# Hybrid RG-LRU, attention and FFN layer: eighth gate pair in Strassen's form, first q and k ahead of the pairs, last gate product behind the second k

## The chip, the cores and the metric

The kernel runs on one core of one Trainium2 chip. The metric is device time in microseconds (us). Before the change three runs took 919.93, 920.62 and 920.92 us; the median is 920.62. The engines are TensorE (PE; PEld is its loading of weights), VectorE (DVE), ScalarE (ACT), GpSimd (POOL) and SyncE (SP). In this kernel SP issues most loads and stores, and POOL the transfers that accumulate.

## The reference

One layer, on x of 512 tokens by 1024 channels in float32. What matters here:

```
h  = RMSNorm_pre(x)
[xa, ga, q, k, v, f, gA, gB] = h @ W_in
A  = GeLU(ga) * RG-LRU(CausalDWConv4(xa))            (width 1280)
B  = ForgettingAttention(q, k, v, f)                 (16 heads of 64)
m  = sigmoid(gA) * (A @ P_A) + sigmoid(gB) * (B @ P_B)
x  = x + RMSNorm_post(m @ W_out)
h  = RMSNorm_pre(x)
u  = CausalDWConv3(h @ W_up); y = (GeLU(u_gate) * u_val) @ W_down
x  = x + RMSNorm_post(y)
```

The attention is causal; the score of token i against token j has the sum of log-sigmoids of f between them added.

## The kernel before

Values are kept transposed, with channels on the 128 partitions and the 512 tokens along the free dimension. Each matmul of float32 accuracy is made of three of the rounded type float32r: a value is split into a rounded part (`wh` of a weight, `hh` of h) and the rest (`wl`, `hl`), and wh by hh (line 218), wh by hl (line 219) and wl by hh (line 220) are accumulated. `project` computes an output tile of 128 channels by 512 tokens in 8 x 3 = 24 such matmuls of 128x512. A weight's path: SP loads it (`raw`, line 166), ACT rounds it (`wh`, line 172), DVE subtracts (`wl`, line 175). `fetch(i)` does this for all weights of a list, `order`, up to number i, `unit(name, ahead)` for the named one and `ahead` more. Four buffers each stand behind raw, wh and wl.

Each of the two gates has eight tiles, ma0 to ma7 for gA and mb0 to mb7 for gB. A gate tile ends with a tanh on ACT (line 865). That of ma is then multiplied into `pa`, the product A @ P_A, on DVE; that of mb is stored to DRAM by SP (`gmb`, line 873) and loaded again much later.

Fourteen of the sixteen tiles are computed in pairs, class `Pair`, with Strassen's seven products (Winograd's form) in place of eight: two tiles are a matrix of two by two blocks (two output tiles, two halves of the 1024 channels), against two halves of the tokens. A product has 12 matmuls of 128x256: 4 wh by rounded h (line 414), 4 wh by the rest of h (line 415) and 4 wl by rounded h (line 417). Products 1, 2 and 3 take plain weights, of which `plain_high` rounds the high part on ACT (`gmh`, line 369); the low part `gml` comes from `plain_low`, which writes the negative high part on ACT (line 360) and lets a transfer of POOL add the raw weight to it (line 361). Products 4 to 7 take sums of weights: `sums` on DVE (`gt`), `sums_hi` rounds them on ACT (`gth`, line 396), `sums_lo` subtracts on DVE (`gtl`). `keep` copies a product out of PSUM on ACT (`gx`, line 421), `add` adds it to another on DVE (line 433). On TensorE a period of one pair has its products 5 and 6, the product 4 of the pair before, its product 3, products 1 and 2 of the next pair, and its product 7. So the last pair leaves one product 4 behind.

Before the pairs, mb6 and mb7 are computed as plain tiles (`gate_tile`). Behind the pairs come q0, k0, the last pair's product 4, and the attention: eight steps p of two heads each. `scores(p)` is a set of matmuls of 64 partitions, two at a time (line 987), each in three rounds (high by high, low k, low q). Its six PSUM banks are read on DVE, which adds the bias B and takes the row maximum (line 996); ACT takes the exponential (line 1001), and `normalise` scales by the reciprocal sum on DVE (lines 1008, 1011). In the code of a step follow the projection of q(p+1), the transposes `pt` of step p-1, the projection of k(p+1), and the product with v, `av`, of step p-1. `halves` splits q and k: h_q and h_k on ACT (line 973), l_q and l_k on DVE (line 974). The bias B is broadcast from DRAM by POOL (line 893) and masked there (line 898).

PSUM has eight banks of 128x512, given out in turn. What sets the order: the code of the gate pairs stands in `manual_schedule`, so there each engine executes its instructions as they are written, up to the last product 4. Outside of it, the framework's scheduler puts each engine's instructions in an order. An engine goes through its own queue in order; `behind` ties the fetch of a weight to the last rounding of `halves`.

Of the kernel before, what the change touches and what calls it, by code (L numbers as in the profile page):

```python
# [19 lines left out]
KD = D // P  # L20
# [43 lines left out]
def kernel(  # L64
# [34 lines left out]
    def bank(name):  # L99
        return pspools[-1].tile([P, 512], F32, tag="ps", name=name)  # L100
# [79 lines left out]
    def cols(w, i):  # L180
        return w[i], (KD, P)
# [5 lines left out]
    order += [(f"v{c}_{u}", w_in[B_V + 4 * c + u], (2, 512)) for c in range(2) for u in range(4)]  # L187
    order += [(f"ga{t}", *cols(w_in, B_GA + t)) for t in range(TR)]
    order += [(f"pa{e}_{i}", w_pa[2 * e + i], (5, P)) for e, i in PA_ORDER]
    order += [(f"mb{e}", *cols(w_in, B_MB + e)) for e in (6, 7)]  # L190
    for p in range(KD):
        order.append((f"q{p}", *cols(w_in, B_Q + p)))
        order.append((f"k{p}", *cols(w_in, B_K + p)))
# [5 lines left out]
    where = {name: i for i, (name, _, _) in enumerate(order)}  # L199
    ready, emitted, special = {}, [0], {}  # L200

    def fetch(i):
        while emitted[0] <= min(i, len(order) - 1):
            n, src, shape = order[emitted[0]]
            w = Split(src, shape, n, special.get(n))
            w.hi()
            w.lo(dve)
            ready[n] = w.parts()
            emitted[0] += 1

    def unit(name, ahead=2):

        i = where[name]
        fetch(i + ahead)
        return ready.pop(name)
# [6 lines left out]
    def project(dst, unit, ah, al, lo=0, hi=S):  # L222
        wh, wl = unit
        for k in range(KD):
            mm3(dst[:, lo:hi], wh[:, k], wl[:, k], ah[:, k, lo:hi], al[:, k, lo:hi], k == 0, k == KD - 1)
# [256 lines left out]
    with ExitStack() as rg:  # L482
# [327 lines left out]
        gdram = ctx.enter_context(tc.tile_pool(name="gdram", bufs=1, space=bass.MemoryType.DRAM))  # L810
        gmb = [gdram.tile([P, S], F32, name=f"gmb{e}") for e in range(KD)]
        gates = Halved("g", lambda e: w_in[(B_MA if e[:2] == "ma" else B_MB) + int(e[2])], hh, hl)
        GP = [(f"{w}{e}", f"{w}{e + 1}") for w, n in (("ma", 8), ("mb", 6)) for e in range(0, n, 2)]
        gp = {}
        dstk = mstk.enter_context(ExitStack())
        sumstk, hfstk, splitstk, bstk = (ExitStack() for _ in range(4))
# [45 lines left out]
    def gate_tanh(name, ps):  # L862
        c = int(name[2]) + (0 if name[:2] == "ma" else KD)
        tg = tgpool.tile([P, S], F32, tag="tg", name=f"tg_{name}")
        act.activation(out=tg, in_=ps, func=AF.Tanh, scale=0.5, bias=hb[:, c : c + 1])
        return tg

    def gate_use(name, tg):
        e = int(name[2])
        if name[:2] == "ma":  # L870
            dve.scalar_tensor_tensor(out=pa[:, e], in0=tg, scalar=1.0, in1=pa[:, e], op0=ALU.add, op1=ALU.mult)
        else:
            nc.sync.dma_start(gmb[e], tg)

    def gate_tile(name, ahead):
        pg = bank(name)
        project(pg, unit(name, ahead), hh, hl)
        gate_use(name, gate_tanh(name, pg))

    def gate_epilogue(b, which, step):  # L880
        if b and step < 2:
            name = b.tiles[which == "c"]
            if step == 0:
                b.tg = getattr(b, "tg", {})
                b.tg[which] = gate_tanh(name, getattr(b, which))
            else:
                gate_use(name, b.tg[which])
# [11 lines left out]
                                   pattern=[[-1, P]], channel_multiplier=1)  # L899
        return bias  # L900

    gate_tile("mb6", 1)
    gate_tile("mb7", 0)
    with ExitStack() as g2:
        spool = g2.enter_context(tc.tile_pool(name="gsums", bufs=1, side="right", reuse_waits="tile"))
        gates.sh = [spool.tile([P, KH, SH], F32R, name=f"gsh{i}") for i in range(4)]
        gates.sl = [spool.tile([P, KH, SH], F32R, name=f"gsl{i}") for i in range(4)]
        gp[1] = Pair(gates, 1, GP[1])
        man = g2.enter_context(ExitStack())
        man.enter_context(tc.manual_schedule())  # L910
        for i, f in enumerate((fq[3], fq[0], fq[2], fq[1])):
            act.copy(gates.sh[i], f)
            sub(gates.sl[i], f, gates.sh[i].bitcast(F32))
        hfstk.close()
        st0pool = splitstk.enter_context(tc.tile_pool(name="gsplit0", bufs=2, side="right", reuse_waits="tile"))
        offset(splitstk, 448, "right")
        st1pool = splitstk.enter_context(tc.tile_pool(name="gsplit1", bufs=2, side="right", reuse_waits="tile"))
        gates.stpools = [st0pool, st1pool]
        none = Nothing()
        p, n = gp[0], gp[1]  # L920
        p.plain_high(0)
        p.plain_high(1)
        p.p12()
        p.p5()
        n.sums(0)
        n.sums(1)
        n.plain_low(0)
        p.keep(2, p.a[:, Y])
        p.add(p.a[:, X], p.a[:, X], 2)
        p.keep(1, p.c[:, X])  # L930
        n.sums_hi(0)
        n.sums_lo(0)
        n.sums_hi(1)
        n.sums_lo(1)
        n.plain_high(0)
        gp[2] = Pair(gates, 2, GP[2])

        def more(j):
            if j + 3 < len(GP):
                gp[j + 3] = Pair(gates, j + 3, GP[j + 3])  # L940
            elif j + 2 < len(GP):
                pass
            else:
                fetch(where[("q0", "k0")[j + 2 - len(GP)]])

        for j in range(len(GP)):
            period(gp[j], gp.get(j - 1), gp.get(j + 1, none), gp.get(j + 2, none), gate_epilogue, lambda: more(j))
            gp.pop(j - 1, None)
        splitstk.close()
        sumstk.close()  # L950
        bpool = bstk.enter_context(tc.tile_pool(name="bias", bufs=2, reuse_waits="tile"))
        bias = prep_alloc(0)
        b = gp.pop(len(GP) - 1)
        b.add(b.c[:, Y], b.a[:, Y], 1)
        b.add(b.c[:, X], b.c[:, X], 0)
        gate_epilogue(b, "c", 0)
        pq = bank("q0")
        project(pq, unit("q0", 0), hh, hl)
        gate_epilogue(b, "c", 1)
        pk = bank("k0")  # L960
        project(pk, unit("k0", 0), hh, hl)
        b.product(4, b.a[:, Y])
        gate_epilogue(b, "a", 0)
        gate_epilogue(b, "a", 1)

    with ExitStack() as at:
        at.enter_context(bstk)
# [98 lines left out]

        rounded = []

        def behind(name):
            with tc.issue_after(rounded[-1].ins):  # L1070
                return unit(name)

        q, k = halves(pq, "q0"), halves(pk, "k0")
        fetch(where["k1"])
        prev = None
        for p in range(KD):
            now = scores(p, q, k, bias)
            if p < KD - 1:
                bias = prep_alloc(p + 1)
                pq = bank(f"q{p + 1}")  # L1080
                project(pq, (unit if p else behind)(f"q{p + 1}"), hh, hl)
            else:
                pb_part(0, range(KD - 2))
            if prev is not None:
                pts = pt(p - 1, prev)
            if p < KD - 1:
                pk = bank(f"k{p + 1}")
                project(pk, behind(f"k{p + 1}"), hh, hl)
                q, k = halves(pq, f"q{p + 1}"), halves(pk, f"k{p + 1}")
            else:  # L1090
                pb_part(1, range(KD - 2))
            if prev is not None:
                av(p - 1, pts)
            normalise(now)
            prev = now
# [612 lines left out]
```

## Time and profile before

| | |
|---|---|
| median of three runs | 920.62 us (919.93 to 920.92) |
| profiled execution | 919.7 us |
| its span | 917.9 us |
| granted TensorE clock, mean | 0.998 |
| TensorE busy | 905.9 us |
| VectorE, ScalarE, GpSimd busy | 721.9, 597.7, 215.8 us |
| mb6 and mb7, plain | 248.27 to 259.15 us |
| first start of the pairs' products | 259.15 us |
| q0 begins, last product 4 begins, scores 0 begins | 327.21, 338.33, 339.86 us |

The profile is one profiled execution; its times count from the start of its span. A line of its timeline has the start, the duration, the engine, the source line, the operation with its output and inputs, and in brackets the idle time of the engine ahead of it with what ended it. TensorE's matmuls overlap, and their ends are modelled, so the time that one takes on the engine is read from the distance of two starts.

### The profile page before, as it was taken

The page shows a single profiled execution, that of the slowest core. Times are in us where ns is not written, and L with a number is a line of the kernel's source. Part 1 is how long each engine was busy: PE and PEld are TensorE (multiplying, and loading weights), DVE is VectorE, ACT ScalarE, POOL GpSimd, SP SyncE. Part 2 cuts the span into 40 slices and gives each one's busy share as a digit, 9 for nine tenths or more (in the row PEclk, how much of TensorE's full clock was granted, in tenths as well). Part 3 has the DMA queues.
Part 4 walks back from the last instruction along what each step waited for, and adds up shares of the span by engine and source line. Part 5 has one row for each costly group of instructions (what it writes and reads, how often), then busy time and mean ns, then how long its engine had stood idle before and what let it go on. Part 6 is the DMA issues. An engine that isn't in the chain of part 4 may idle for free.

```text
span 917.9 us, 15845 instructions
## 1 busy us (share of the span) xinstructions
PE 905.9 (99%) x5870; PEld 803.2 (88%) x5870; DVE 721.9 (79%) x1190; ACT 597.7 (65%) x1034; POOL 215.8 (24%) x279
## 2 busy tenths in 40 slices
PE   8999999999999999999999999999999999999997
PEld 7988888878899987888888889999999999978886
DVE  5966369638767647888868588899999999889897
ACT  7555495433467646677654477788888888677664
POOL 4134345444111112112104200132323223100000
PEclk9999999999999999999999999999999999999999
DMA  7767689989877776235424654378888888799764
GB/s 276 241 209 210 166 207 250 273 218 194 195 184 184 182 260 247 104 126 179 143 83 153 205 185 158 93 194 208 219 230 214 238 199 211 222 372 326 243 204 147
DMA packets 71760, 187.07 MB, mean 204 GB/s; under 512 B 7233, under 2 KB 27761, under 8 KB 71298
## 3 DMA queue, kind: packets, MB, share of 16 engines
q1 hardware_dynamic: 47648, 127.72, 41.9%
q0 software_dynamic: 23888, 58.20, 29.0%
q8 instruction: 46, 0.75, 0.3%
q14 instruction: 32, 0.26, 0.1%
q10 hardware_dynamic: 146, 0.14, 0.0%
HBM read 150.69 MB, written 35.73 MB: 203 GB/s over the span
## 4 chain that ended last, share of the span: by engine, by line
PE 89%; DMA 4%; DVE 4%; issue 1%; ACT 1%; POOL 0%; SPq 0%; DVEq 0%; ACTq 0%; POOLq 0%
PE up L417 7%; PE up L414 6%; PE up L415 6%; PE dn L1420 4%; PE dn L1418 4%; PE dn L1419 4%; DMA ml<-raw_up 2%; PE ga L218 2%; PE ga L219 2%; PE ga L220 2%; PE q L218 2%; PE k L218 2%; PE pb L218 2%; PE wo L1142 2%; PE k L220 2%; PE pb L219 2%
## 5 line engine op out<-in xcount | busy, mean ns | idle before, releaser
L1300 DVE SCALAR_TENSOR_TENSOR u<-up,cpt,u 128x511 f32<-128x511 f32 x96 | 71.2, 744 | 2.6 <-ACT u L1294 0.9
L361 POOL DMA_DIRECT2D ml<-raw_up x41 | 35.2, 858 | 154.2 <-ACT ml L360 91.1
L1418 PE MATMUL dn<-wh_dn,ah 128*128 128x512 f32 (+1 forms) x180 | 67.6, 376 | 0.2 <-ACT ah L1386 0.2
L1420 PE MATMUL dn<-wh_dn,al 128*128 128x512 f32 (+1 forms) x180 | 67.7, 376 | 0.0
L1419 PE MATMUL dn<-wl_dn,ah 128*128 128x512 f32 (+1 forms) x180 | 67.6, 375 | 0.0
L414 PE MATMUL up<-sh,th 128*128 128x256 f32 x252 | 60.2, 276 | 0.0
L415 PE MATMUL up<-sl,th 128*128 128x256 f32 x252 | 60.2, 276 | 0.0
L175 DVE TENSOR_TENSOR wl_dn<-raw_dn,wh_dn 128x1024 fp32r<-128x1024 f32 x42 | 51.5, 1226 | 9.2 <-ACT wh_dn L172 9.1
L172 ACT CAST wh_dn<-raw_dn 128x1024 fp32r<-128x1024 f32 x42 | 44.1, 1050 | 17.8 <-issue 8.0
L325 DVE TENSOR_TENSOR tl<-t,th 128x1024 fp32r<-128x1024 f32 x42 | 51.0, 1217 | 0.0
L1294 ACT ACTIVATE u<-up,cpt 128x512 f32<-128x512 f32 x48 | 37.0, 779 | 21.4 <-PE up L417 11.6
L415 PEld LDWEIGHTS up<-sl,th 128*128 128x128 f32 x252 | 47.3, 188 | 0.0
L414 PEld LDWEIGHTS up<-sh,th 128*128 128x128 f32 x252 | 47.3, 188 | 0.0
L396 ACT CAST th<-t 128x1024 fp32r<-128x1024 f32 x42 | 43.8, 1045 | 3.8 <-DVE t L325 0.8
L1308 POOL TENSOR_TENSOR yf<-u,u 128x512 f32<-128x512 f32 x23 | 29.9, 1298 | 63.6 <-issue 44.0
L414 PE MATMUL up<-h2h,mh 128*128 128x256 f32 x168 | 40.2, 276 | 0.0
L415 PE MATMUL up<-h2l,mh 128*128 128x256 f32 x168 | 40.2, 276 | 0.0
L1420 PEld LDWEIGHTS dn<-wh_dn,al 128*128 128x128 f32 x180 | 33.9, 188 | 7.0 <-DVE al L325 0.8
L1418 PEld LDWEIGHTS dn<-wh_dn,ah 128*128 128x128 f32 x180 | 33.9, 188 | 6.6 <-ACT ah L1386 0.6
L1419 PEld LDWEIGHTS dn<-wl_dn,ah 128*128 128x128 f32 x180 | 33.9, 188 | 6.1
L417 PE MATMUL up<-sh,tl 128*128 128x256 f32 x252 | 38.8, 276 | 0.0
L433 DVE TENSOR_TENSOR up<-up,x 128x256 f32<-128x256 f32 x63 | 27.1, 432 | 13.8 <-PE up L417 9.4
(719 smaller groups left out, 3226.3 us busy)
## 6 DMA issues: line engine op xcount, KB each, us to landing
raw_up<-in_w_up_dram SPq DMA_DIRECT2D x48, 512.0 KB, 4.9
td<-in_w_down_dram POOLq DMA_DIRECT2D x36, 512.0 KB, 7.0
raw_dn<-td SPq DMA_DIRECT2D x24, 512.0 KB, 5.2
B<-cnd POOLq DMA_DIRECT2D x16, 640.0 KB, 5.7
ml<-raw_up POOLq DMA_DIRECT2D x20, 512.0 KB, 5.4
raw_dn<-in_w_down_dram SPq DMA_DIRECT2D x18, 512.0 KB, 4.3
raw_wo<-in_w_out_dram SPq DMA_DIRECT2D x16, 512.0 KB, 3.6
td<-td POOLq DMA_DIRECT2D x12, 512.0 KB, 11.2
```

Source lines behind the costliest of these rows:

```text
L172: act.copy(self.wh, self.raw)
L175: engine.tensor_tensor(out=self.wl, in0=self.raw, in1=self.wh.bitcast(F32), op=ALU.subtract)
L218: pe.matmul(dst, ah, bh, start=first, stop=False)
L325: dve.tensor_tensor(out=out, in0=a, in1=b, op=ALU.subtract)
L396: act.copy(self.th[i], self.t[i])
L414: pe.matmul(dst, wh[:, k], ah[:, k], start=first and k == 0, stop=False, skip_group_check=True)
L415: pe.matmul(dst, wh[:, k], al[:, k], start=False, stop=False, skip_group_check=True)
L417: pe.matmul(dst, wl[:, k], ah[:, k], start=False, stop=k == KH - 1, skip_group_check=True)
L1300: dve.scalar_tensor_tensor(out=c[:, s:], in0=ps[:, : S - s], scalar=col(C_CFW + 3 * e + j), in1=c[:, s:], op0=ALU.mult, op1=ALU.add)
L1418: pe.matmul(d[:, x], ah[:, k, tok], wh[:, k, x], start=first, stop=False, skip_group_check=True)
L1419: pe.matmul(d[:, x], ah[:, k, tok], wl[:, k, x], start=False, stop=False, skip_group_check=True)
L1420: pe.matmul(d[:, x], al[:, k, tok], wh[:, k, x], start=False, stop=last, skip_group_check=True)
```

## The change

The pairs become eight: mb6 and mb7 are the last pair, and `gate_tile` goes. In their place ahead of the pairs q0 and k0 are projected and held in two PSUM banks (`held`) until the attention. At the head of the pairs ACT's instructions for pair 1 are written in another order: the rounding of its plain weights (`plain_high(0)`) and of its sums (`sums_hi`) stands ahead of the copies `keep`. At the tail, q1 is projected directly behind the last product 7, then scores 0, k1, and the last pair's product 4 behind k1, with its tanh and store. The weight of q1 is fetched in the last period but one, that of k1 behind the first tanh of the last pair, and q2 behind the rounding of q0 and k0 (`behind`). The lines of the changed kernel are up to 8 lower in number.

```diff
-    order += [(f"mb{e}", *cols(w_in, B_MB + e)) for e in (6, 7)]
     for p in range(KD):
         order.append((f"q{p}", *cols(w_in, B_Q + p)))
         order.append((f"k{p}", *cols(w_in, B_K + p)))
...
-        GP = [(f"{w}{e}", f"{w}{e + 1}") for w, n in (("ma", 8), ("mb", 6)) for e in range(0, n, 2)]
+        GP = [(f"{w}{e}", f"{w}{e + 1}") for w in ("ma", "mb") for e in range(0, 8, 2)]
...
-    def gate_tile(name, ahead):
-        pg = bank(name)
-        project(pg, unit(name, ahead), hh, hl)
-        gate_use(name, gate_tanh(name, pg))
+    def held(name, ahead):
+        ps = bank(name)
+        project(ps, unit(name, ahead), hh, hl)
+        return ps
...
-    gate_tile("mb6", 1)
-    gate_tile("mb7", 0)
+    pq, pk = held("q0", 1), held("k0", 0)
...
         n.plain_low(0)
+        n.plain_high(0)
+        n.sums_hi(0)
+        n.sums_hi(1)
         p.keep(2, p.a[:, Y])
         p.add(p.a[:, X], p.a[:, X], 2)
         p.keep(1, p.c[:, X])
-        n.sums_hi(0)
         n.sums_lo(0)
-        n.sums_hi(1)
         n.sums_lo(1)
-        n.plain_high(0)
...
-            else:
-                fetch(where[("q0", "k0")[j + 2 - len(GP)]])
+            elif j + 2 == len(GP):
+                fetch(where["q1"])
...
         gate_epilogue(b, "c", 0)
-        pq = bank("q0")
-        project(pq, unit("q0", 0), hh, hl)
+        fetch(where["k1"])
         gate_epilogue(b, "c", 1)
-        pk = bank("k0")
-        project(pk, unit("k0", 0), hh, hl)
-        b.product(4, b.a[:, Y])
-        gate_epilogue(b, "a", 0)
-        gate_epilogue(b, "a", 1)
...
-        def behind(name):
+        def behind(name, ahead=2):
             with tc.issue_after(rounded[-1].ins):
-                return unit(name)
+                return unit(name, ahead)
...
-        fetch(where["k1"])
         prev = None
         for p in range(KD):
+            if p == 0:
+                pq = held("q1", 1)
             now = scores(p, q, k, bias)
             if p < KD - 1:
                 bias = prep_alloc(p + 1)
+            if 0 < p < KD - 1:
                 pq = bank(f"q{p + 1}")
-                project(pq, (unit if p else behind)(f"q{p + 1}"), hh, hl)
-            else:
+                project(pq, (unit if p > 1 else behind)(f"q{p + 1}"), hh, hl)
+            elif p:
                 pb_part(0, range(KD - 2))
...
-                project(pk, behind(f"k{p + 1}"), hh, hl)
+                project(pk, behind(f"k{p + 1}", 2 if p else 0), hh, hl)
...
+            if p == 0:
+                b.product(4, b.a[:, Y])
+                gate_epilogue(b, "a", 0)
+                gate_epilogue(b, "a", 1)
```

Three places of the queues. First ScalarE at the head of the pairs, before; in the names the first number is the part and the second the pair (gmh0_1 is part 0 of pair 1):

```order
L360 ACTIVATE gml0_1_2576<-raw_ma2_2499 128x1024
L421 COPY gx2_0_2579<-ma0_2532 128x256
L421 COPY gx1_0_2582<-ma1_2557 128x256
L396 CAST gth0_1_2584<-gt0_1_2570 128x1024
L396 CAST gth1_1_2588<-gt1_1_2573 128x1024
L369 CAST gmh0_1_2592<-raw_ma2_2499 128x1024
L421 COPY gx0_0_2610<-ma0_2532 128x256
```

and after:

```order
L368 CAST gmh0_1_2573<-raw_ma2_2493 128x1024
L395 CAST gth0_1_2575<-gt0_1_2564 128x1024
L395 CAST gth1_1_2577<-gt1_1_2567 128x1024
L420 COPY gx2_0_2579<-ma0_2526 128x256
L420 COPY gx1_0_2582<-ma1_2551 128x256
L420 COPY gx0_0_2604<-ma0_2526 128x256
```

The three roundings moved ahead of the copies, and gmh0_1 ahead of the two gth.

Second, TensorE at the tail, the first row of each group of matmuls (of a product, a projection, a set of scores), before; gth0 carries products 5 and 7, gth1 products 6 and 4, gmh1 product 3:

```order
L414 MATMUL mb5_3316<-gsh3_2494,gmh1_6_3208 128x256
L414 MATMUL mb4_3268<-gsh2_2493,gth0_6_3229 128x256
L218 MATMUL q0_3434<-hh_114,wh_q0_3299 128x512
L218 MATMUL k0_3460<-hh_114,wh_k0_3378 128x512
L414 MATMUL mb4_3268<-hh_114,gth1_6_3253 128x256
L987 MATMUL s0c_3527<-h_k0_3509,h_q0_3505 128x512
L218 MATMUL q1_3605<-hh_114,wh_q1_3514 128x512
L218 MATMUL k1_3636<-hh_114,wh_k1_3520 128x512
L987 MATMUL s2c_3687<-h_k1_3671,h_q1_3667 128x512
L218 MATMUL q2_3765<-hh_114,wh_q2_3607 128x512
```

and after:

```order
L413 MATMUL mb7_3439<-gsh3_2488,gmh1_7_3331 128x256
L413 MATMUL mb6_3391<-gsh2_2487,gth0_7_3352 128x256
L217 MATMUL q1_3571<-hh_114,wh_q1_3422 128x512
L979 MATMUL s0c_3598<-h_k0_3567,h_q0_3563 128x512
L217 MATMUL k1_3676<-hh_114,wh_k1_3552 128x512
L413 MATMUL mb6_3391<-hh_114,gth1_7_3376 128x256
L979 MATMUL s2c_3736<-h_k1_3705,h_q1_3701 128x512
L217 MATMUL q2_3814<-hh_114,wh_q2_3816 128x512
```

q0 and k0 are gone from here, q1 stands ahead of scores 0, and product 4 between k1 and scores 1.

Third, VectorE at the same place, from l_k0 to the first maximum of scores 1, one row of each kind, before (P, mx is a maximum, P<-P,sm a scaling):

```order
L974 TENSOR_TENSOR l_k0_3510<-k0_3460,h_k0_3509 128x512
L175 TENSOR_TENSOR wl_q2_3608<-raw_q2_3606,wh_q2_3607 128x1024
L996 ISA P0_3555,mx0_3556<-s0c_3527,B0_3402 128x512
L175 TENSOR_TENSOR wl_k2_3639<-raw_k2_3637,wh_k2_3638 128x1024
L996 ISA P1_3566,mx1_3567<-s1a_3528,B1_3404 128x128
L1011 TENSOR_SCALAR P1_3566<-P1_3566,sm1_3568 128x256
L175 TENSOR_TENSOR wl_q3_3768<-raw_q3_3766,wh_q3_3767 128x1024
L974 TENSOR_TENSOR l_q1_3668<-q1_3605,h_q1_3667 128x512
L974 TENSOR_TENSOR l_k1_3672<-k1_3636,h_k1_3671 128x512
L175 TENSOR_TENSOR wl_k3_3865<-raw_k3_3863,wh_k3_3864 128x1024
L996 ISA P2_3715,mx2_3716<-s2c_3687,B2_3577 128x512
```

and after:

```order
L966 TENSOR_TENSOR l_k0_3568<-k0_2457,h_k0_3567 128x512
L175 TENSOR_TENSOR wl_k1_3553<-raw_k1_3551,wh_k1_3552 128x1024
L988 ISA P0_3626,mx0_3627<-s0c_3598,B0_3519 128x512
L988 ISA P1_3637,mx1_3638<-s1a_3599,B1_3521 128x128
L966 TENSOR_TENSOR l_q1_3702<-q1_3571,h_q1_3701 128x512
L1003 TENSOR_SCALAR P1_3637<-P1_3637,sm1_3639 128x256
L966 TENSOR_TENSOR l_k1_3706<-k1_3676,h_k1_3705 128x512
L175 TENSOR_TENSOR wl_q2_3817<-raw_q2_3815,wh_q2_3816 128x1024
L988 ISA P2_3764,mx2_3765<-s2c_3736,B2_3648 128x512
```

Each weight stands later against the scores than before: wl_k1 ahead of the first maximum, where wl_q2 stood, and wl_q2 behind l_k1, where wl_k3 stood.

## The prediction

> **What bounds the kernel now.** I read the page first: the span, the busy shares and the chain that ended last.
>
> ```profile
> span 917.9 us, 15845 instructions
> PE 905.9 (99%) x5870; PEld 803.2 (88%) x5870; DVE 721.9 (79%) x1190; ACT 597.7 (65%) x1034; POOL 215.8 (24%) x279
> ...
> PE 89%; DMA 4%; DVE 4%; issue 1%; ACT 1%; POOL 0%; SPq 0%; DVEq 0%; ACTq 0%; POOLq 0%
> ...
> L172 ACT CAST wh_dn<-raw_dn 128x1024 fp32r<-128x1024 f32 x42 | 44.1, 1050 | 17.8 <-issue 8.0
> ...
> L414 PEld LDWEIGHTS up<-sh,th 128*128 128x128 f32 x252 | 47.3, 188 | 0.0
> ```
>
> TensorE is busy for 99% of the span and carries 89% of the chain. A change is worth the matmuls that it takes from TensorE, and the few places where TensorE stands still. So I went to TensorE's timeline where the change works, and took differences of start times, since the ends are modelled.
>
> ```profile
> 248.27 0.39 PE L218 MATMUL mb<-hh,wh_mb 128*128 128x512 f32 x1
> ...
> 259.15 0.28 PE L414 MATMUL ma<-hh,gmh 128*128 128x256 f32 x1
> ...
> 265.74 0.63 PE L417 MATMUL ma<-gsh,gml 128*128 128x256 f32 x4
> 266.85 0.38 PE L414 MATMUL ma<-hh,gmh 128*128 128x256 f32 x1 [0.48 <-ACT gmh L369]
> 267.07 0.28 PE L415 MATMUL ma<-hl,gmh 128*128 128x256 f32 x1
> ...
> 276.73 0.28 PE L414 MATMUL ma<-hh,gmh 128*128 128x256 f32 x1
> ...
> 286.51 0.28 PE L414 MATMUL ma<-hh,gmh 128*128 128x256 f32 x1
> ...
> 327.21 0.39 PE L218 MATMUL q<-hh,wh_q 128*128 128x512 f32 x1
> ...
> 338.33 0.28 PE L414 MATMUL mb<-hh,gth 128*128 128x256 f32 x1
> ...
> 339.86 0.50 PE L987 MATMUL s0c<-h_k,h_q 64*128 64x512 f32 x1
> ...
> 341.91 0.50 PE L218 MATMUL q<-hh,wh_q 128*128 128x512 f32 x1
> ...
> 352.68 0.39 PE L220 MATMUL k<-hh,wl_k 128*128 128x512 f32 x1
> 353.80 0.49 PE L987 MATMUL s2c<-h_k,h_q 64*128 64x512 f32 x1 [0.73 <-ACT h_k L973]
> ...
> 356.18 0.50 PE L218 MATMUL q<-hh,wh_q 128*128 128x512 f32 x1
> ...
> 371.36 0.49 PE L987 MATMUL s4c<-h_k,h_q 64*128 64x512 f32 x1
> ...
> 373.43 0.50 PE L218 MATMUL q<-hh,wh_q 128*128 128x512 f32 x1
> ```
>
> The reader is to see five stretches in it. mb6 and mb7 as plain tiles run from 248.27 to 259.15, 10.88 us for 48 matmuls, 226.7 ns each. A whole pair, from one pair's product 1 to the next one's, takes 286.51 - 276.73 = 9.78 us for 84 matmuls, 116.4 ns each. The four products at 265.74 are followed by a wait for ScalarE. q0 and k0 take 327.21 to 338.33, 11.12 us, and the last product 4 takes 338.33 to 339.86, 1.53 us. And behind k1 TensorE waits for the rounding of k1 at 353.80.
>
> **The change part by part, against the profiled execution of 919.7 us.** That is 0.92 below the median of 920.62, so I work out a difference and add it to the median.
>
> *Front.* q0 and k0 are 48 matmuls of the same shapes as mb6 and mb7 and stand in their place, with their weights in the same place of the fetch order: 10.88 for 10.88, no difference. The two banks that they hold leave six of eight to the pairs. A pair takes two, and the third pair after it needs them again, 3 x 9.78 = 29 us later, while its own last product and its tanh come within two periods, 20 us: nothing, with nothing on either side.
>
> *Rounding order at the front.* ScalarE before:
>
> ```profile
> 262.17 0.37 ACT L421 COPY gx<-ma 128x256 f32<-128x256 f32 x1 [2.13 <-PE ma L417]
> 263.58 0.37 ACT L421 COPY gx<-ma 128x256 f32<-128x256 f32 x1 [1.04 <-PE ma L417]
> 263.85 2.00 ACT L396 CAST gth<-gt 128x1024 fp32r<-128x1024 f32 x2
> 265.76 1.04 ACT L369 CAST gmh<-raw_ma 128x1024 fp32r<-128x1024 f32 x1
> ...
> 258.15 0.90 POOL L361 DMA_DIRECT2D gml<-raw_ma  x1 [16.60 <-ACT gml L360]
> ...
> DMA to landing us min/median/max: 4.0/6.1/8.1
> ```
>
> The cast that TensorE waits for starts only at 265.76, behind two copies that wait for TensorE and two other casts, although ScalarE idles 2.13 us ahead of the first copy. The four matmuls at 265.74 are 113 ns apart, so the next was due at 266.19; it came at 266.85 (0.66 late) and the one after it 0.22 on, not 0.11. Moved ahead of the copies, the three casts fall into that idle stretch: -0.75. What is late next is the low part of the same product, an accumulating transfer issued at 258.15. At the longest landing of these transfers (8.1, the last row, which is of tile gml around here) it is there at 266.25, and its first matmul is due 8 x 0.113 after 266.19, at 267.1: 0.85 spare. The bounds are 0 and -0.77; I take -0.75.
>
> *Eighth pair.* One period more, +9.78. It also puts two accumulating transfers on POOL's queue, one period behind those of the pair before, as for every pair; were one late, the period takes a few tenths more. With the plain tiles' place taken by q0 and k0, what it replaces is those two at the tail, -11.12 (10.88 for the matmuls, 0.24 for k0's late weights, next fence): -1.34 together.
>
> *Product 4 behind k1.* Its 1.53 us only move. But they move to where TensorE stands still:
>
> ```profile
> PE s2c L987 <- ACT h_k L973: 0.7, 1, 0.7
> ...
> PEld k L220 <- DVE wl_k L175: 0.4, 1, 0.4
> ```
>
> k1's last matmul started at 352.68, the next was due at 352.91, and scores 1 came at 353.80: 0.89. Then scores 1 took 356.18 - 353.80 = 2.38 where scores 2, which has av0 ahead of it as cover, took 373.43 - 371.36 = 2.07: another 0.31. Of these 1.20 I leave 0.10 for the change of shape from q1 to scores 0, now without product 4 between: -1.10. The bounds are 0 (another wait ends last) and -1.20.
>
> *What is given back on VectorE.* Its queue before:
>
> ```profile
> 341.25 0.68 DVE L996 CUSTOM_DVE_ANT_0 P<-s0c,B 128x512 f32<-128x512 f32 x1
> ...
> 346.18 0.18 DVE L1008 RECIPROCAL sm<-sm 128x4 f32<-128x4 f32 x1 [0.43 <-ACT P L1001]
> ...
> 347.79 1.27 DVE L1011 TENSOR_SCALAR P<-P,sm 128x512 f32<-128x512 f32 x4
> 348.98 1.22 DVE L175 TENSOR_TENSOR wl_q<-raw_q,wh_q 128x1024 fp32r<-128x1024 f32 x1
> ...
> 355.87 0.68 DVE L996 CUSTOM_DVE_ANT_0 P<-s2c,B 128x512 f32<-128x512 f32 x1
> ...
> 360.13 0.18 DVE L1008 RECIPROCAL sm<-sm 128x4 f32<-128x4 f32 x1 [0.88 <-ACT P L1001]
> ...
> 369.66 0.69 DVE L974 TENSOR_TENSOR l_k<-k,h_k 128x512 fp32r<-128x512 f32 x1 [1.74 <-ACT h_k L973]
> ```
>
> Before, 353.80 - 339.86 = 13.94 us lay between the starts of scores 0 and scores 1. Now there are 2.05 + 5.44 + 1.53, about 9.1, for the same row maxima and scalings, and l_k1 stands behind all of them. From the first maximum to the end of the scalings it took 348.98 - 341.25 = 7.7 us. T is the start of scores 0. The first maximum can start at T + 1.15 (half of the 2.05), the scalings end at T + 8.9 and l_k1 at T + 9.6, less up to 1.1 because one weight subtraction of 1.2 no longer stands among the maxima. Scores 1 wants l_k1 with its second round, at T + 9.5. So 0 to 0.2 here. In the next period VectorE has wl_k2, wl_q3, wl_k3 and wl_q4 ahead of l_k2 instead of wl_q4 alone, 3 x 1.15 = 3.4 us more. Against that stand 1.74 idle ahead of l_k2, 0.88 idle ahead of the reciprocal, and about 0.4 by which the first maximum of scores 1 can start earlier (355.87 is 2.07 behind the start of scores 1; now it waits for wl_q2, behind l_k1, 1.6 behind it). That leaves 0.4, which TensorE pays once, at av0 or scores 2; for both places I take 0.4, between 0 and 0.8.
>
> *The late fetch.* raw_k1 is now issued behind the store of gmb4, and its subtraction wl_k1 stands ahead of the first maximum on VectorE. k1's bank is one that this maximum frees. Before, raw_k0 stood behind such a store in the last period:
>
> ```profile
> 325.86 0.38 SPq L166 DMA_DIRECT2D raw_k<-in_w_in_dram  x1
> ...
> L166 SPq DMA_DIRECT2D raw_k<-in_w_in_dram x5: 328/373/382, 325.9 to 343.7; - x5
> ...
> DMA to landing us min/median/max: 4.7/5.1/8.1
> ...
> DMA to landing us min/median/max: 4.6/6.0/8.8
> ```
>
> It was issued 327.21 - 325.86 = 1.35 us before the last product 7 ended. The second row and the landing below it are of tile raw_k, the last of raw_q, both of the stretch from 320 to 345. To cost nothing, wl_k1 must be done by T + 1.15, and T is q1's 5.45 behind the last product 7. Rounding (the 1050 ns of the page's row of line 172) and subtraction take 1.05 + 1.2, so the load may take 1.35 + 5.45 + 1.15 - 2.25 = 5.7 us. At the two medians it costs 0 and 0.3, at the two longest 2.4 and 3.1. I take 0.2, nearer to the medians.
>
> **Sum.** 0 - 0.75 - 1.34 - 1.10 + 0.4 + 0.2 = -2.6 us: 920.62 - 2.6 = 918.0.
>
> **Rivals.** (1) *VectorE becomes the bound* over scores 0 to scores 2: l_k1 late, then l_k2. For it speaks that the same work has 4.8 us less room; against it that VectorE still idles 1.74 us in that stretch. If half of these 4.8 came to the path, -3.2 + 2.4 = -0.8: 919.8.
>
> (2) *One gain is not there*, since another wait takes the place of the one removed: at 266 the accumulating transfer (spare 0.85), or at k1 VectorE. The sum is then -1.5 to -1.9, about 918.9.
>
> (3) *Slower: raw_k1 lands late.* Each us beyond 5.7 holds wl_k1, behind it the first maximum, behind that k1's bank and so TensorE, and nothing overtakes it. The sum without it, -2.8, is eaten at 8.5 us and the time is 0.2% up at about 10.3: at 11 us, 920.62 - 2.8 + 5.3 = 923.1. The rows show no load over 8.8 there, but the rotation of the queues differs; against it, these are 512 KB loads with two more right behind.
>
> (4) *Short matmuls bound by weight loads.* If a 128x256 matmul cost its weight load, 188 ns by the page, a pair would take 84 x 188 = 15.8 us and the change 6.0 more, 924. The rows say 116.4 ns, loads overlapped, in each pair. The Trainium skill has a rule in this direction (TensorE: Matmul & The Clock Gate, Back-to-back issue gap): in a stream of weight loads and matmuls, 512 columns sustain some 131 ns and 128 columns some 81, so that a shorter matmul saves less than its share. By an estimate of 98 ns for 256 columns from that page, a pair would be 84 x 98 = 8.2 us against 48 x 131 = 6.3 for two plain tiles, a loss of 1.9 instead of the gain of 1.1, and the sum would come out near +0.4, no change. The trace disagrees: 226.7 and 116.4 ns, nearly half.
>
> **How the numbers follow.** Forecast as summed, -1.9 to -3.3: 0.60. Rival 1: 0.16. Rival 2: 0.08. Rival 3: 0.12, of it 0.05 within 0.2% and 0.07 beyond. Rival 4: 0.01. Something that shows only in the changed trace, such as loads and accumulating transfers falling together in later stages: 0.03, slower. 0.2% is 1.84 us, about what a measurement of this kernel tells from no change. Faster by more: the forecast and half of rival 2, 0.64. Within: rival 1, the other half of 2, the milder part of 3, 0.25. Slower: 0.11. The range starts at all gains without loss, -3.2, and half a us for a better fit of the loads, 916.9, and reaches over rival 1 to the milder half of rival 3, 920.9; it leaves out about 0.15.
>
> **What the profile afterwards would show.** No wait of TensorE for gmh near 266, and the next matmul at the 113 ns step. An eighth period of 9.8 us. q1 directly behind the last product 7. Behind k1 the twelve matmuls of product 4 and no wait for h_k in scores 1; instead perhaps short waits for l_k there and at scores 2. raw_k1's landing under 6 us, or else a wait ahead of k1. The prediction is wrong if waits of TensorE for wl_k, l_k or PTl between scores 0 and scores 2 add up to more than 1.5 us, or if stages that the change leaves alone become longer.

## The result and the profile after

Six runs of the changed kernel took 914.89 to 918.74 us, median 916.63; six of the kernel before in the same series 919.93 to 920.92, median 920.60. The ratio is 0.9959, with a 95% interval of 0.9948 to 0.9970: faster by 0.41% (0.30 to 0.52). The forecast was 918.0 with a range from 916.9: the direction holds, the time lies 0.27 us below the range. In a later series with more runs the ratio was 0.9967 (0.9957 to 0.9977), with 916.34 for the changed kernel (12 runs) and 919.81 for the one before (29 runs).

The page of the changed kernel, its span and busy times:

```profile
span 914.5 us, 15941 instructions
PE 904.9 (99%) x5906; PEld 805.5 (88%) x5906; DVE 725.6 (79%) x1197; ACT 601.7 (66%) x1041; POOL 217.6 (24%) x281
```

TensorE is busy 1.0 us less than before and idle 2.4 us less. TensorE's timeline at the places that the prediction used (in the changed kernel line 217 is the 218 of before, 413 is 414, 979 is 987):

```profile
247.75 0.39 PE L217 MATMUL q<-hh,wh_q 128*128 128x512 f32 x1
...
258.66 0.28 PE L413 MATMUL ma<-hh,gmh 128*128 128x256 f32 x1
...
265.25 0.64 PE L416 MATMUL ma<-gsh,gml 128*128 128x256 f32 x4
265.73 0.28 PE L413 MATMUL ma<-hh,gmh 128*128 128x256 f32 x1
...
335.44 0.39 PE L217 MATMUL q<-hh,wh_q 128*128 128x512 f32 x1
...
340.99 0.49 PE L979 MATMUL s0c<-h_k,h_q 64*128 64x512 f32 x1
...
343.06 0.50 PE L217 MATMUL k<-hh,wh_k 128*128 128x512 f32 x1
...
348.62 0.28 PE L413 MATMUL mb<-hh,gth 128*128 128x256 f32 x1
...
350.14 0.49 PE L979 MATMUL s2c<-h_k,h_q 64*128 64x512 f32 x1
...
352.20 0.50 PE L217 MATMUL q<-hh,wh_q 128*128 128x512 f32 x1
...
367.38 0.49 PE L979 MATMUL s4c<-h_k,h_q 64*128 64x512 f32 x1
```

The reader is to see that no row has a wait. At 265.73 the matmul follows the four ahead of it without a gap. q1 starts at 335.44, directly behind the last product 7. Scores 1 take 352.20 - 350.14 = 2.06 us, as scores 2 did before. From here on the two kernels do the same in the same time: q2 to scores 2 takes 15.18 us in both (356.18 to 371.36, and 352.20 to 367.38).

So the change is measured best on one stretch: from the first matmul that stands behind the product A @ P_A (of mb6 before, of q0 after) to the first matmul of q2. Before it took 356.18 - 248.27 = 107.91 us, after 352.20 - 247.75 = 104.45: -3.46. By parts: the front 10.88 and 10.91; the pairs' products up to the last product 7 68.06 (259.15 to 327.21) and 76.78 (258.66 to 335.44), +8.72; from there to q2 28.97 and 16.76, -12.21. Everything outside of the stretch takes 917.9 - 107.9 = 810.0 and 914.5 - 104.5 = 810.0 us.

### The profile page after: what moved, and what is told of

Same layout as the page of the kernel before. It is cut to its first block, busy times and chain, and to the rows that moved or that the text cites. A ratio compares the mean times of both kernels' runs of the same rounds, so it can differ in the third digit from the quotient of the medians.

```text
span 914.5 us, 15941 instructions
## 1 busy us (share of the span) xinstructions
PE 904.9 (99%) x5906; PEld 805.5 (88%) x5906; DVE 725.6 (79%) x1197; ACT 601.7 (66%) x1041; POOL 217.6 (24%) x281
## 4 chain that ended last, share of the span: by engine, by line
PE 92%; DVE 4%; DMA 1%; issue 1%; ACT 1%; POOL 0%; DVEq 0%; POOLq 0%; ACTq 0%
PE up L416 7%; PE up L414 7%; PE up L413 7%; PE dn L1418 4%; PE dn L1416 4%; PE dn L1417 4%; PE pa L218 2%; PE ga L219 2%; PE pa L217 2%; PE ga L218 2%; PE pa L219 2%; PE ga L217 2%; PE k L217 2%; PE q L217 2%; PE pb L217 2%; PE pb L218 2%
```

## The experiments

Single runs of one kernel differ by some 4 us, more than the parts of the change are worth. The stretch does not. The table has it for each kernel, from the profiled execution: start of the first matmul of q0 or mb6, start of q2's first matmul, their difference, and the rest of the span outside; then the median with its number of runs, and the ratio to the kernel before in the same series. In a_p4early, b_p4late, a_plain67 and a_plain67b one more edit, left out of the diffs below, ties each projection and each set of scores of the attention to the TensorE group written before it (`chain`), and in b_p4late and the two plain versions product 4 too, so that TensorE keeps the written order; the two plain versions also bring back `gate_tile` and the weights of mb6 and mb7 in `order`. The tie itself costs nothing that the trace shows: q1 to q2 takes 354.28 - 337.54 = 16.74 us in a_plain67b and 16.76 in the changed kernel.

| kernel | start | q2 | stretch | rest | median (runs) | ratio |
|---|---|---|---|---|---|---|
| before | 248.27 | 356.18 | 107.91 | 810.0 | 920.60 (6) | |
| after | 247.75 | 352.20 | 104.45 | 810.0 | 916.63 (6) | 0.9948 to 0.9970 |
| a_again | 248.27 | 352.83 | 104.57 | 809.5 | 916.34 (12) | 0.9957 to 0.9977 |
| a_oldround | 248.09 | 353.41 | 105.33 | 810.7 | 916.25 (9) | 0.9955 to 0.9977 |
| a_p4early | 249.58 | 356.20 | 106.62 | 810.3 | 918.53 (12) | 0.9979 to 0.9998 |
| a_plain67 | 248.61 | 359.21 | 110.61 | 812.4 | 922.89 (9) | 1.0019 to 1.0043 |
| b_newround | 248.95 | 356.17 | 107.22 | 811.2 | 919.94 (12) | 0.9976 to 0.9997 |
| b_p4late | 247.97 | 356.36 | 108.39 | 810.0 | 920.45 (12) | 0.9987 to 1.0010 |
| a_latek1 | 248.22 | 353.70 | 105.48 | 808.6 | 916.91 (11) | 0.9952 to 0.9977 |
| a_dve12 | 248.07 | 354.94 | 106.87 | 809.4 | 917.22 (11) | 0.9950 to 0.9976 |
| a_plain67b | 248.51 | 354.28 | 105.77 | 811.4 | 918.53 (10) | 0.9972 to 0.9990 |
| a_frontlate | 247.97 | 353.80 | 105.83 | 810.2 | 917.28 (5) | 0.9946 to 0.9976 |
| a_frontlate_fix | 249.47 | 354.64 | 105.17 | 811.1 | 918.01 (10) | 0.9963 to 0.9983 |
| a_fix | 249.88 | 354.47 | 104.59 | 811.3 | 917.05 (5) | 0.9952 to 0.9977 |

**The base again (a_again).** No edit.

> The changed kernel once more, as the base of the others of its set and for its spread (its six times ran from 914.9 to 918.7 us, the kernel before from 919.9 to 920.9). Theory A (the gain lies in the stretch that the change touches, the spread elsewhere): from the first matmul of q0 to the first of q2 it takes 104.4 to 104.6 us again, whatever the whole execution takes; the median is within 1 us of 916.6. Theory B (part of the gain comes from stretches that the change does not touch, by other places of buffers): the stretches before q0 or behind q2 are 0.3 us or more shorter than before in this execution too.

The stretch is 104.57 us. The rest of the span goes from 808.6 to 812.4 us over all fourteen executions; its mean is 810.4 for the three kernels made from the one before (810.0, 811.2, 810.0) and 810.4 for the eleven made from the changed one. Behind q2 this execution is 0.5 us shorter than the one before, as theory B asked for, but that is within this spread. So theory A, as far as three and eleven executions can tell: the gain lies in the stretch, 3.34 to 3.46 us, and the spread of single runs outside of it.

**Old order of roundings (a_oldround).**

```diff
         n.plain_low(0)
-        n.plain_high(0)
-        n.sums_hi(0)
-        n.sums_hi(1)
         p.keep(2, p.a[:, Y])
         p.add(p.a[:, X], p.a[:, X], 2)
         p.keep(1, p.c[:, X])
+        n.sums_hi(0)
         n.sums_lo(0)
+        n.sums_hi(1)
         n.sums_lo(1)
+        n.plain_high(0)
```

> The changed kernel with the roundings of pair 1 behind the copies again. Theory A: TensorE waits for gmh at the end of the first period again, 0.75 us, and the low parts of the later pairs are issued 1.3 us later, so that one is late by 0.2: stretch from q0 to q2 105.3 to 105.5, time up by 0.9. Theory B (another wait was close behind and the order is worth little): stretch up by 0.3 at most.

TensorE's timeline of this kernel:

```profile
265.74 0.63 PE L416 MATMUL ma<-gsh,gml 128*128 128x256 f32 x4
266.85 0.38 PE L413 MATMUL ma<-hh,gmh 128*128 128x256 f32 x1 [0.48 <-ACT gmh L368]
```

The wait is back, to the hundredth where it stood before, and the stretch is 105.33, 0.76 to 0.88 longer than in the two executions of the changed kernel. The wait itself is 0.75 of it (a step of 0.76 and one of 0.22, where 0.113 were due); in this execution q0 also has a late weight, 0.11. A late low part at the fourth pair was not seen, so that wait of before (0.2 us) does not hang on the order of the roundings. The median alone (916.25) would have shown nothing.

**Only the new order of roundings (b_newround).** The same lines, changed the other way in the kernel before.

> The kernel before with only the new order of roundings at the head of the pairs. Theory A: the wait for gmh at the end of the first period goes (0.75 us) and, since the low parts of the later pairs are then issued 1.3 us earlier, the 0.2 us at the fourth pair too: from the first matmul of mb6 to the first of q2 106.9 to 107.2 us instead of 107.9. Rival (the low part's transfer takes its place): 107.6 or more.

The stretch is 107.22, 0.69 shorter, just outside theory A's 106.9 to 107.2. The wait for gmh is gone, but the low part's transfer, issued at 258.91, landed 9.1 us later, and takes 0.31 of the gain (TensorE, this kernel):

```profile
267.72 0.28 PE L415 MATMUL ma<-hl,gmh 128*128 128x256 f32 x1
268.03 0.50 PE L417 MATMUL ma<-hh,gml 128*128 128x256 f32 x2
```

The step here is 0.31 where it should be 0.113, and the next 0.22. So the transfer does stand close behind, as the prediction had it, with a spare that its landing can use up.

**Product 4 ahead of q1 (a_p4early).**

```diff
         gate_epilogue(b, "c", 1)
+        b.product(4, b.a[:, Y])
+        gate_epilogue(b, "a", 0)
+        gate_epilogue(b, "a", 1)
...
-            if p == 0:
-                b.product(4, b.a[:, Y])
-                gate_epilogue(b, "a", 0)
-                gate_epilogue(b, "a", 1)
```

> The changed kernel with the last product 4 directly behind the last product 7, ahead of q1, TensorE's order otherwise kept. Theory A (k1's rounding on ScalarE is what it covers): TensorE waits for h_k in scores 1, and the stretch from q0 to q2 grows by 1.1. Theory B (VectorE sets the end of this place, since l_k1 stands behind the scalings): TensorE waits for l_k in the second round of scores 1, nearly all of the 1.5 us is lost, 1.35 to 1.5.

The stretch is 106.62, 2.1 longer: more than either theory. The waits of TensorE in this kernel say why:

```profile
PE s2c L982 <- ACT h_k L968: 0.7, 1, 0.7
PE mb L413 <- DVE mb L432: 0.6, 1, 0.6
PE s2c L982 <- DVE l_k L969: 0.2, 1, 0.2
```

and its timeline at the product itself:

```profile
336.86 0.62 PE L416 MATMUL mb<-gsh,gtl 128*128 128x256 f32 x4
338.08 0.39 PE L413 MATMUL mb<-hh,gth 128*128 128x256 f32 x1 [0.60 <-DVE mb L432]
```

Directly behind product 7, product 4 waits for VectorE's addition, which has to read the bank that it accumulates into: 338.08 - 336.86 = 1.22 for four steps of 0.113, and the step behind it 0.22, so 0.87 in all. Neither theory had thought of this. Behind k1 the waits for h_k and l_k come back: scores 1 start 0.9 late (k1 takes 6.45 us to them, not 5.56) and take 2.52 instead of 2.06. That is 1.35 us, theory B's size, of which the larger part is theory A's wait for the rounding.

**Product 4 behind k1 in the kernel before (b_p4late).**

```diff
-        b.product(4, b.a[:, Y])
-        gate_epilogue(b, "a", 0)
-        gate_epilogue(b, "a", 1)
...
                 q, k = halves(pq, f"q{p + 1}"), halves(pk, f"k{p + 1}")
             else:
                 pb_part(1, range(KD - 2))
+            if p == 0:
+                b.product(4, b.a[:, Y])
+                gate_epilogue(b, "a", 0)
+                gate_epilogue(b, "a", 1)
```

> The kernel before with only the last product 4 moved behind k1, TensorE's order otherwise kept. Theory A (product 4 covers a rounding wherever it stands, and before it covered that of k0): the wait for h_k in scores 1 goes, one for h_k appears ahead of scores 0, and the stretch to q2 stays within 0.3 us of 107.9; the gain of 1.1 needs q0 and k0 ahead of the pairs. The prediction's own reading (the move alone is worth 1.1): 106.8.

The stretch is 108.39, not shorter but 0.5 longer: far from the prediction's own reading, and 0.2 beyond theory A's bound. TensorE's waits between the pairs and q2:

```profile
PE s0c L984 <- ACT h_k L970: 0.7, 1, 0.7
PE s2c L984 <- DVE l_k L971: 0.6, 1, 0.6
```

The wait for the rounding of k has gone from k1 to k0, which product 4 covered before, and l_k1 is late as well. By itself the move gains nothing. It gains because q0 and k0, projected ahead of the pairs, need no cover any more.

**Plain tiles for mb6 and mb7 (a_plain67, a_plain67b).** The first version fetched q1 behind mb6:

```diff
-        GP = [(f"{w}{e}", f"{w}{e + 1}") for w in ("ma", "mb") for e in range(0, 8, 2)]
+        GP = [(f"{w}{e}", f"{w}{e + 1}") for w, n in (("ma", 8), ("mb", 6)) for e in range(0, n, 2)]
...
         gate_epilogue(b, "c", 0)
-        fetch(where["k1"])
+        gate_tile("mb6", 0)
         gate_epilogue(b, "c", 1)
+        fetch(where["q1"])
+        gate_tile("mb7", 1)
+        fetch(where["k1"])
```

> The changed kernel with seven pairs, mb6 and mb7 as plain tiles behind the last product 7 and ahead of q1; the last product 4 is that of the seventh pair, behind k1. Theory A (a short matmul costs half a long one): 48 x 226.7 = 10.9 us in place of a period of 9.7, stretch up by 1.1 to 1.4, with up to 0.3 more for late weights. Rival (short matmuls sustain less than twice the rate): stretch shorter, by up to 1.9.

The stretch is 110.61. It is not the price of the plain tiles: TensorE waits for the weight of q1, as its list of waits says.

```profile
PE q L219 <- ACT wh_q L172: 2.2, 1, 2.2
```

mb6 and mb7 were done at 337.9; q1 started at 340.26 and stayed slow until its parts were there (7.46 us instead of 5.5). The second version fetches q1 ahead of mb6 and k1 behind it:

```diff
-        gate_tile("mb6", 0)
-        gate_epilogue(b, "c", 1)
         fetch(where["q1"])
-        gate_tile("mb7", 1)
+        gate_epilogue(b, "c", 1)
+        gate_tile("mb6", 0)
         fetch(where["k1"])
+        gate_tile("mb7", 0)
```

> The changed kernel with seven pairs, mb6 and mb7 as plain tiles behind the last product 7, and the weight of q1 now fetched ahead of mb6, so that no load is late at q1. Theory A: 48 x 226.7 = 10.9 us instead of a period of 9.7, so from the first matmul of q0 to the first of q2 105.6 to 106.0 instead of 104.5, and 0.35 more where the low part at the fourth pair is late as it was with seven pairs before. Rival (short matmuls sustain less than twice the rate of long ones): 103.5 or less.

105.77: 1.20 to 1.32 us longer than with the eighth pair, of it 0.11 at a low part in the fourth pair. The two plain tiles took 10.90 us for 48 matmuls, from mb6 to q1 on TensorE:

```profile
326.64 0.39 PE L219 MATMUL mb<-hh,wh_mb 128*128 128x512 f32 x1
...
337.54 0.39 PE L219 MATMUL q<-hh,wh_q 128*128 128x512 f32 x1
```

So a pair costs 9.7 to 9.8, as its period says (324.31 - 314.54 = 9.77 us between the first products 1 of the last two pairs of the changed kernel). Of these two forms, 48 matmuls of 512 columns at 227 ns against 84 of 256 at 116, the price goes with the columns. The rule of the Trainium skill that was weighed (TensorE: Matmul & The Clock Gate, Back-to-back issue gap) would, by the estimate made from it, have made the plain version about 1.9 us shorter; the measurement decides against it here.

**A later load of k1's weight (a_latek1).**

```diff
-        fetch(where["k1"])
         gate_epilogue(b, "c", 1)
+        fetch(where["k1"])
```

> The changed kernel with the load of k1's weight issued behind the store of gmb7, some 3.8 us later; the scheduler then puts wl_k1 behind the first maximum. Theory A (in the changed kernel wl_k1 was ready 1.4 us ahead of its use): the load lands 4.3 us after its issue, wl_k1 is ready 0.9 to 1.3 us after k1's third matmul was due, TensorE waits for wl_k in k1, and the stretch from q0 to q2 is 105.4 to 105.9. Rival (the wait is given back, since VectorE's queue had room behind): under 104.9.

105.48, as theory A has it: about 1.0 lost. TensorE's timeline in k1 and in scores 1:

```profile
343.89 0.39 PE L218 MATMUL k<-hl,wh_k 128*128 128x512 f32 x1
344.48 0.50 PE L219 MATMUL k<-hh,wl_k 128*128 128x512 f32 x1 [0.20 <-DVE wl_k L175]
...
351.13 0.49 PE L979 MATMUL s2c<-h_k,h_q 64*128 64x512 f32 x1
...
351.87 0.50 PE L979 MATMUL s2c<-l_k,h_q 64*128 64x512 f32 x1 [0.25 <-DVE l_k L966]
```

The step behind the second matmul of k1 is 0.59 instead of 0.23, and the second round of scores 1 comes 0.74 behind the first, not 0.33: VectorE, busy with wl_k1 among the maxima, is late with l_k1 too.

**More work on VectorE ahead of l_k1 (a_dve12).**

```diff
-            dve.tensor_tensor(out=lo, in0=ps, in1=hi.bitcast(F32), op=ALU.subtract)
+            for _ in range(3 if name == "q1" else 1):
+                dve.tensor_tensor(out=lo, in0=ps, in1=hi.bitcast(F32), op=ALU.subtract)
```

> The changed kernel with l_q1 written three times over, 1.2 us more on VectorE between the maxima of scores 0 and l_k1. Theory A (the changed kernel has only 0.1 to 0.2 us to spare at l_k1): 0.3 of it fills VectorE's wait for the exponentials, the rest, 0.6 to 0.9 us, becomes a wait for l_k in the second round of scores 1, and nothing is lost later: stretch 105.1 to 105.5. Rival (the scores' other rounds and the exponentials leave room): under 104.8. Where it also costs at av0 or scores 2, the stretch from q2 to scores 2 is over its 15.2 us.

106.87: twice too much for the theory. The timeline of TensorE has two waits, and only one is at the place of the edit:

```profile
262.75 0.63 PE L416 MATMUL ma<-gsh,gtl 128*128 128x256 f32 x4
264.41 0.39 PE L413 MATMUL ma<-gsh,gth 128*128 128x256 f32 x1 [1.03 <-DVE ma L432]
...
351.74 0.49 PE L980 MATMUL s2c<-h_k,h_q 64*128 64x512 f32 x1
...
353.12 0.49 PE L980 MATMUL s2c<-l_k,h_q 64*128 64x512 f32 x1 [0.89 <-DVE l_k L967]
```

In scores 1 the second round comes 1.38 behind the first instead of 0.33: 1.05 of the 1.2 us go to the path, so l_k1 has 0.15 us to spare in the changed kernel. That is more than the 0.6 to 0.9 of theory A, since VectorE still waits 0.31 us for the exponentials as in the changed kernel, and does not fill that wait. Behind scores 1 nothing more is lost (q2 to scores 2 takes 15.19). The other 1.3 us are lost ahead of the edit, in the first period. There, in this execution, ScalarE was late:

```profile
260.97 1.05 ACT L395 CAST gth<-gt 128x1024 fp32r<-128x1024 f32 x1 [0.73 <-DVE gt L324]
262.58 1.05 ACT L395 CAST gth<-gt 128x1024 fp32r<-128x1024 f32 x1 [0.56 <-DVE gt L324]
263.53 0.64 ACT L420 COPY gx<-ma 128x256 f32<-128x256 f32 x2
```

and for comparison the same of the changed kernel:

```profile
259.08 1.05 ACT L395 CAST gth<-gt 128x1024 fp32r<-128x1024 f32 x1 [0.74 <-DVE gt L324]
260.69 1.05 ACT L395 CAST gth<-gt 128x1024 fp32r<-128x1024 f32 x1 [0.55 <-DVE gt L324]
261.68 0.37 ACT L420 COPY gx<-ma 128x256 f32<-128x256 f32 x1
```

The pairs start at 258.99 and 258.66, so the copy that the addition needs is 1.5 us later against them. It stands behind the two roundings, and these wait for VectorE's sums. VectorE is late in turn because wl_k0 is, and that goes back to GpSimd:

```profile
241.29 9.40 POOL L149 COPY tick<-wh_pa 128x1 f32<-128x1 f32 x1
...
250.72 1.05 ACT L172 CAST wh_k<-raw_k 128x1024 fp32r<-128x1024 f32 x1 [2.31 <-POOL tick L149]
...
251.80 1.23 DVE L175 TENSOR_TENSOR wl_k<-raw_k,wh_k 128x1024 fp32r<-128x1024 f32 x1 [1.16 <-ACT wh_k L172]
```

GpSimd's copy of one column of wh_pa took 9.40 us here and 0.60 to 1.59 us at this place in the other thirteen executions, and the rounding wh_k0 started as it ended. Why it took so long stays open. It lies far ahead of the edit, so these 1.3 us are put down to this execution; without them the stretch would be 105.57, just above theory A's 105.5.

**That delay, made on purpose (a_frontlate, a_frontlate_fix, a_fix).** The first kernel writes wl_k0 twice (the first part of the diff), which puts VectorE back by 1.2 us ahead of the pairs; the second one has the other part too, the copy ahead of the second rounding; the third has the other part alone.

```diff
-            w.lo(dve)
+            for _ in range(2 if n == "k0" else 1):
+                w.lo(dve)
...
         n.sums_hi(0)
-        n.sums_hi(1)
         p.keep(2, p.a[:, Y])
         p.add(p.a[:, X], p.a[:, X], 2)
+        n.sums_hi(1)
         p.keep(1, p.c[:, X])
```

> The changed kernel with wl_k0 written twice, so that VectorE's work ahead of the pairs, and with it all roundings of pair 1 on ScalarE, is 1.2 us later. It imitates the profiled execution of the kernel with the lengthened VectorE queue, in which wl_k0 waited 1.2 us longer for its rounding and TensorE then waited 1.2 us for an addition behind product 5's copies. Theory A (in the new order the copies gx stand behind roundings that wait for VectorE's sums, with 0.2 to 0.3 us to spare): TensorE waits 0.9 to 1.1 us for the addition in the first period, stretch from q0 to q2 105.4 to 105.6. Rival (that wait came from a load or another queue of that execution): 104.4 to 104.7.

> The same delay of 1.2 us, with the first copy gx ahead of the second gth in ScalarE's code. Theory A: the copy no longer waits for the second rounding, the wait for the addition goes, stretch 104.4 to 104.7. Rival: as in the run before, 105.4 or more.

> The changed kernel with the first copy gx ahead of the second gth, without the delay. Theory A: no difference in an execution in which nothing is late, stretch 104.4 to 104.6, time within 1 us of that of the changed kernel. Rival (the second gth then makes something late): over 104.8.

With the delay 105.83, and the waits of TensorE are

```profile
PE ma L414 <- DVE ma L433: 0.7, 1, 0.7
PE ma L417 <- DMA gml<-raw_ma: 0.2, 1, 0.2
```

With the copy ahead 105.17, and the first of the two is gone:

```profile
PE ma L417 <- DMA gml<-raw_ma: 0.3, 1, 0.3
```

Without the delay 104.59, as the changed kernel. So the wait seen in the lengthened queue's execution is the copy behind the roundings, theory A, 1.0 us of it; the low part, late by the same delay, then takes 0.5 to 0.6 that theory A did not reckon. So 105.83 lies above theory A's range, and 105.17 between theory A's and the rival's. Under this delay the order with the copy ahead is the safer one, by 0.66 us. It is no faster where nothing is late: 917.05 us, ratio 0.9952 to 0.9977, against 0.9957 to 0.9977 for the changed kernel. No version beat the changed kernel beyond the spread.

## Why the prediction was right or wrong

*Front, 0.* Right: 10.91 for 10.88.

*Rounding order, -0.75.* Right in size: the matmul at 265.73 follows without a gap, and undoing the order costs 0.76 to 0.88. That the low part stands next in line was right as well. Its spare of 0.85 was worked out from one landing of 8.1; a landing of 8.9 uses it up (a_again: 0.11 lost at 267.19), and one of 9.1 takes 0.31 (b_newround). Not foreseen was that the order puts the copies behind roundings that wait for VectorE, with some 0.2 us to spare (a_frontlate: a copy 1.24 us later cost 1.02).

*Eighth pair for q0 and k0, -1.34.* Right: a plain version of mb6 and mb7 costs 1.20 to 1.32 more, 1.09 to 1.21 without the late low part (forecast 10.88 - 9.78 = 1.10). The other 0.24 of the term, k0's late weights, is a matter of the execution: k0 has none in the changed kernel (258.66 - 253.22 = 5.44 us), but none in b_newround either (338.04 - 332.60 = 5.44).

*Product 4 behind k1, -1.10.* The size is right: from the start of the last product 4 (before) or of q1 (after) to q2 it was 356.18 - 338.33 = 17.85 and is 352.20 - 335.44 = 16.76, -1.09. The reason was told too simply. Product 4 covers a wait wherever it stands, and the gain needs q0 and k0 out of the way; alone it gave nothing. The early place for it would also have met the addition, 0.87.

*What is given back on VectorE, +0.4.* This step failed: nothing was given back, since q2 to scores 2 takes 15.18 us before and after. For l_k1 its bounds 0 to 0.2 hold (its 2.05 + 5.44 + 1.53 is 9.02 and not 9.1, but scores 0 to scores 1 took 350.14 - 340.99 = 9.15); VectorE's timeline after:

```profile
342.10 0.69 DVE L988 CUSTOM_DVE_ANT_0 P<-s0c,B 128x512 f32<-128x512 f32 x1 [1.35 <-PE s1c L979]
...
349.64 0.68 DVE L966 TENSOR_TENSOR l_k<-k,h_k 128x512 fp32r<-128x512 f32 x1
...
365.81 0.68 DVE L966 TENSOR_TENSOR l_k<-k,h_k 128x512 fp32r<-128x512 f32 x1
```

l_k1 ends at 350.32, and the second round of scores 1 is due 0.33 behind 350.14, at 350.47: 0.15 to spare, and nothing lost. For l_k2 the 0.4 was wrong. It set 3.4 us of added work against VectorE's idle time alone. That time was indeed filled: from l_k1 to l_k2 VectorE's timeline has no idle time in brackets any more, and l_k2 ends 366.49 - 352.20 = 14.29 us behind the start of q2, before 14.17. But l_k2 had ended, before, at 369.66 + 0.69 = 370.35, while the second round of scores 2 was due at 371.36 + 0.33 = 371.69: another 1.34 of spare, which the step left out, in no bracket of an idle time, since it lies between the end of one instruction and the start of its reader on another engine. After, l_k2 ends at 366.49 and is due at 367.71, and 1.2 is left.

*The late fetch, +0.2.* This term was not paid either. ScalarE's rounding of the load, after:

```profile
338.44 1.05 ACT L172 CAST wh_k<-raw_k 128x1024 fp32r<-128x1024 f32 x1 [1.04 <-DMA raw_k<-in_w_in_dram]
```

The deadline of 5.7 us was right, the load was not late: issued at 334.10, 1.34 us ahead of product 7's end as worked out, it landed at 338.4, where ScalarE's rounding starts, after 4.3 us, and VectorE then waited 1.35 us for scores 0 (the row at 342.10). The 0.2 was a mean over landings of other stretches, put into a sum that was to be the likeliest. A load 3.75 us later lost 1.0.

*The sum.* The two terms are 0.6 us of the forecast, and neither was paid. Without them it was 0 - 0.75 - 1.34 - 1.10 = -3.19; the stretch gave -3.46 and, in the second execution, -3.34. Of the remaining 0.15 to 0.27, 0.19 is a wait for a low part at the fourth pair, which the execution before had and the two after had not.

*The range.* It started from the median of three runs, 920.62. In the later series, of 22 to 33 runs on three chips, the medians of the kernel before are 919.81, 920.46 and 920.43, so 0.2 to 0.8 lower; the range allowed for the terms, with no part for the base. The summed gains without a give-back, -3.2, from the mean of these three medians, 920.2, give 917.0. The last 0.4 us to the measured 916.63 has no cause that the runs show: the medians of the first series lie 3.97 us apart, 0.5 more than the stretch gives, within an interval of 2.8 to 4.8, and in the later series 3.47. Taken from 920.62, these 3.47 would give 917.15, inside the range. So the two terms are what the forecast had wrong; that the time fell outside the range as well is in part chance.

*The rivals.* None came about. VectorE did not become the bound, though it stands 0.15 us from it at l_k1. The transfer next in line took part of a gain in a kernel with one part of the change alone (0.31), and 0.11 in the second execution of the changed kernel. The late load is real as a mechanism, but dearer in the forecast than on the chip: issued 3.75 us later against scores 0, it landed at 341.90, which made wl_k1 some 1.5 us late by the prediction's reckoning; 1.0 was lost, with wl_k1 behind the first maximum.

## What to carry to other kernels

A piece of work that waits for nothing is worth the wait that it covers; ask of a move which wait it uncovers where it stood, and which of its own inputs it then stands next to. The spare of a result is the time from its end to the start of its reader, and idle time on the engine that makes it is only part of that; a give-back is to be summed only where this spare is used up. Where single runs spread by more than the parts of a change, measure the parts on the distance of two starts around them.

## What was not expected of the hardware

In all fourteen executions q2 to scores 2 took 15.17 to 15.22 us, and the whole stretch 104.45 and 104.57 in the two of the changed kernel, while the rest of the span spread from 808.6 to 812.4 us with the same work in it. The transfers that accumulate gml took 3.2 to 10.1 us from issue to landing over these executions, for the same 512 and 256 KB. And one copy of a single column on GpSimd took 9.40 us in one execution, and 0.60 to 1.59 us in the thirteen others.
